# A decoder trunk on one core: the loads of its down projection in a written order, two homes for the sum Q + B21 and its load on GpSimd's queue, raw blocks in three loads

## The chip, the cores and the metric

The kernel runs on one NeuronCore of a Trainium2 chip. The metric is the device time of one execution in microseconds (us), and the time of a kernel is the median of its timed runs. A profile is one more execution, recorded instruction by instruction; its span runs from the first to the last recorded work.

Names: PE is the matrix engine (PEld loads its weights), DVE the vector engine, ACT the scalar engine, POOL is GpSimd, SP the engine that issues most DMAs. A home is a buffer in SBUF. Each engine takes its instructions in order; an engine that issues DMAs also does so in order, so a DMA that waits for its home holds back all that its engine issues behind it.

## The reference, cut to what matters

One layer of a hybrid decoder on 272 rows (16 meta tokens and 256 of the sequence) with a model width of 2048, in float32: a mixer of retention and mLSTM heads with its output projection, and then a gated FFN with a causal convolution of width 3. The change touches only the last product:

```python
u = rmsnorm(h, norm_ffn)
up = causal_dwconv(u @ w_up, ffn_conv_w, ffn_conv_b)   # 2048 -> 2 x 5632
gate, val = jnp.split(up, [FFN_DIM], axis=-1)
h = h + (jax.nn.silu(gate) * val) @ w_down             # 5632 -> 2048
return rmsnorm(h, norm_final)[:, N_META:]
```

## The kernel before, in words

**Precision.** Every weight and activation is split into a high part (a cast on ACT, tile `whi`) and a low part (a subtraction on DVE, tile `wlo`), and each product is three matmuls: high by high, high by low, low by high. `whi` and `wlo` have five buffers each.

**Two halves.** The FFN goes twice through an up projection (weights `wu`) and a down projection (weights `wd`), each time for half of the 5632 rows. In the trace the down projection of half 0 lies between 719 and 845 us, that of half 1 between 1098 and 1226 us.

**Blocks and steps.** A down projection has two blocks, b = 0 and b = 2, of 1024 columns each (two column blocks j of 512), and a block takes 11 steps q of 256 rows of `wd`. A plain step (q = 0, 9, 10; tile product L819 to L822) loads two weight tiles of 128 x 1024 (512 KB) from `wd`, splits them and has 12 matmuls of 512 columns for each j. A fast step (q = 1 to 8; `seven`, L824 to L855) is a Strassen-like scheme: seven products, 21 matmuls. For it the host gives `wd7`, four quarter matrices per step. The last block of half 1 takes its steps in the order 0, 1, 6, 2, 7, 3, 4, 5, 8, 9, 10, with 6 to 10 plain, and 7 to 10 in two parts.

**What a fast step reads.** Its raw block is a home `left[0]` or `left[1]` by turns (they lie in the tile `hT`), with four quarters of 128 x 512: quarter 0 is Q, a sum of quarter matrices, and 1 to 3 come from `wd7`. `ta` (L838, on DVE) is quarter 0 less quarters 1 and 2. `tb` is Q + B21. Q and Q + B21 are summed in DRAM ahead of time, by accumulating DMAs on POOL's queue during the up projection (class `Early`, L193 to L216; tile `kept`). Then four pairs of splits feed the seven products in this order: quarters 2 and 3; quarters 0 and 1; `ta`; `tb`. The weights' `whi` come from L766 (ACT), the `wlo` from L768 (DVE).

**Homes.** Beside `left` there are four homes for raw weights, `wraw0` and `wraw1`, two buffers each, shared by the up projection's tiles, the plain steps (one side or the other) and `ta` and `tb`, which take the two buffers of `wraw1`. So `ta` and `tb` have one home each.

**Ends of a block.** After the last fast step `share` adds and subtracts the products that belong to several outputs, and `onto` (L871) adds tiles `x` onto the hidden state `hn` by four DMAs on POOL's queue; four more follow when the plain sums leave PSUM (L964). At the end of half 1 the kernel loads `gfin` (1 MB, POOL's queue) and copies `a21`, which lies in the same memory as `left[1]` (L905), before the steps begin.

**Order.** The code is written step by step, and the framework's scheduler puts the instructions of each engine in order by simulated times; an `issue_after` pins one instruction behind another. In the code of before, the loads of a fast step are written inside `seven` (L833: quarter 0; L834: quarters 1 to 3; L837: `tb`), all on SP, and the plain loads (L126, by `load_step`) a step ahead; nothing is pinned there, and where they stand on SP is the scheduler's.

Of the kernel before, what the change touches and what calls it, by code (L numbers as in the profile page):

```python
# [13 lines left out]
ALU = mybir.AluOpType  # L14
PSUM = bass.MemoryType.PSUM

P = 128
# [68 lines left out]
def trunk(ctx: ExitStack, tc: tile.TileContext, io, out: bass.AP):  # L86
# [34 lines left out]
    def load_raw(src, shape, side=None):  # L121

        nonlocal last_load, loads
        raw = raw_home(shape, loads % 4 // 2 if side is None else side)
        loads += 1
        last_load = nc.sync.dma_start(raw, src)  # L126
        return raw
# [629 lines left out]
    for half in range(2):  # L757
# [66 lines left out]
        def seven(b, q, cs, ps, first, last, after, norm):  # L824


            nonlocal turn
            f = FAST.index(q)
            raw = left[turn]
            turn = 1 - turn  # L830

            kept = early[b, half * NQD + q].kept
            nc.sync.dma_start(raw[:, 0, :], kept[:, 0, :])  # L833
            nc.sync.dma_start(raw[:, 1:4, :], io["wd7"][b // 2, half * NQD + q][:, 1:4, :])  # L834
            ta, tb = (raw_home([P, 2, 512], 1) for _ in range(2))

            nc.sync.dma_start(tb[:, 0, :], kept[:, 1, :])  # L837
            nc.vector.tensor_tensor(out=ta, in0=raw[:, 0:1, :].to_broadcast([P, 2, 512]), in1=raw[:, 1:3, :], op=ALU.subtract)  # L838
            copied = None
            for w, to in (  # L840
# [3 lines left out]
                (tb[:, 0:1, :], ((A22, cs[1, 0], False, False),)),  # L844
# [24 lines left out]
        def onto(tt, b, x):  # L869

            nc.gpsimd.dma_start(block(tt, b), x, accum_op=ALU.add)  # L871

        def share(ps, b, final):
# [16 lines left out]
            onto(1, b + 1, x5)  # L890
# [17 lines left out]
        def load_step(b, q, side):  # L908

            return load_raw(io["wd"][b, half * NQD + q], [P, 2, 512], side)  # L910
# [7 lines left out]
        for b in (0, 2):  # L918
# [11 lines left out]
            raws = {}  # L930

            def load_plain(q):
                side = 0 if q == plain[0] or q not in steps[steps.index(fast[-1]) + 2 :] else plain.index(q) % 2
                for j in range(1 if q in alone else 2):
                    raws[q, j] = load_step(b + j, q, side)

            for n, q in enumerate(steps):

                if q in plain and (q, 0) not in raws:
                    load_plain(q)  # L940
                if n + 1 < len(steps) and steps[n + 1] in plain and q in fast:
                    load_plain(steps[n + 1])
                if q in fast:
# [4 lines left out]
                    if q == fast[-1]:  # L948
                        with tc.high_priority() if final else nullcontext():
                            share(ps, b, final)  # L950
                    continue
                for j in range(2):
                    if j == 1 and q in alone:
                        continue
                    w = split_step(raws[q, j])
                    for tt in range(2):
# [125 lines left out]
```

## Time and profile before

| | us |
|---|---|
| median of 3 runs | 1231.93 (1230.17 to 1232.15) |
| the profiled execution | 1235.55 |
| its span | 1233.8 |
| mean granted clock of PE (share of full speed) | 0.994 |
| down projection, half 0 | 719.2 to 844.6 |
| down projection, half 1 | 1098.2 to 1225.6 |

A row of a timeline gives start, duration, engine, line, operation, output and input tiles and, in brackets, how long the engine sat idle before it and what it waited for; rows of one kind in sequence are merged (x2). A row of the waits gives an engine's line and what it waited for: total us, times, longest. "SPq" and "POOLq" are the engines' queues of DMAs; the time of such a row is the issue and not the transfer.

### The profile page before, as it was taken

How to read it: one execution, taken by the hardware profiler on the slowest of the kernel's cores; microseconds unless marked ns; L12 is line 12 of the kernel's file. 1: busy time of each engine (PE TensorE's matmuls, PEld its weight loads, DVE VectorE, ACT ScalarE, POOL GpSimd, SP SyncE). 2: the span in 40 equal slices, each digit the busy share in tenths (PEclk: the TensorE clock that was granted, in tenths of full speed). 3: DMA queues.
4: the chain of work that ended last, by engine and by line, in shares of the span. 5: the costliest groups of instructions: out<-in, count | busy, mean ns of one | idle time of the engine just before them, and what ended most of it. 6: DMA issues, size and time to landing. Idle time of an engine off the chain costs nothing.

```text
span 1233.8 us, 22950 instructions
## 1 busy us (share of the span) xinstructions
PE 1207.8 (98%) x8947; PEld 1152.5 (93%) x8947; DVE 946.9 (77%) x1378; ACT 711.2 (58%) x973; POOL 248.8 (20%) x332
## 2 busy tenths in 40 slices
PE   9999999999999999999999999998999999999897
PEld 9999999999999999999999987678999999986686
DVE  8967878777766767788888789795877777769687
ACT  8747656565557546555555555654655555556564
POOL 0100022222222331232223100103232232200212
PEclk9999999999999999999999999999999999999899
DMA  7765677877786888787778857969988777856855
GB/s 273 273 205 163 209 227 224 229 230 219 229 226 187 254 235 246 218 235 231 223 231 230 264 180 239 247 234 284 284 247 232 225 229 229 219 185 219 236 202 180
DMA packets 101774, 281.64 MB, mean 228 GB/s; under 512 B 16160, under 2 KB 20384, under 8 KB 101536
## 3 DMA queue, kind: packets, MB, share of 16 engines
q1 hardware_dynamic: 84016, 246.66, 59.1%
q0 software_dynamic: 17072, 32.65, 16.7%
q8 instruction: 70, 1.15, 0.4%
q10 hardware_dynamic: 576, 0.85, 0.2%
q14 instruction: 40, 0.33, 0.1%
HBM read 268.59 MB, written 42.47 MB: 252 GB/s over the span
## 4 chain that ended last, share of the span: by engine, by line
PE 88%; DMA 6%; ACT 2%; DVE 2%; issue 1%; SPq 0%; DVEq 0%; ACTq 0%
PE mmps L149 25%; PE mmps L150 25%; PE mmps L152 25%; DMA wraw<-in_wd 2%; DMA wraw<-kept 2%; PE atps L819 1%; PE atps L820 1%; PE atps L822 1%; PE mmps L852 1%; PE mmps L853 1%; ACT whi L766 1%; PE mmps L855 1%; PE atps L852 1%; PE atps L853 1%; PE atps L855 1%
## 5 line engine op out<-in xcount | busy, mean ns | idle before, releaser
L140 ACT CAST whi<-wraw 128x1024 fp32r<-128x1024 f32 x346 | 361.7, 1048 | 356.5 <-PE mmps L150 217.4
L142 DVE TENSOR_TENSOR wlo<-wraw,whi 128x1024 fp32r<-128x1024 f32 x346 | 430.8, 1247 | 107.1 <-ACT whi L140 103.1
L149 PE MATMUL mmps<-uh,whi 128*128 128x258 f32 x1408 | 345.2, 283 | 1.8 <-ACT whi L140 1.8
L150 PE MATMUL mmps<-ul,whi 128*128 128x258 f32 x1408 | 344.9, 281 | 0.0
L149 PEld LDWEIGHTS mmps<-uh,whi 128*128 128x128 f32 x1408 | 265.2, 188 | 2.3 <-ACT whi L140 2.3
L150 PEld LDWEIGHTS mmps<-ul,whi 128*128 128x128 f32 x1408 | 266.5, 189 | 0.0
L149 PE MATMUL mmps<-xh,whi 128*128 128x272 f32 (+2 forms) x864 | 219.8, 288 | 0.0
L150 PE MATMUL mmps<-xl,whi 128*128 128x272 f32 (+2 forms) x864 | 218.4, 285 | 0.0
L152 PE MATMUL mmps<-uh,wlo 128*128 128x258 f32 x1408 | 197.9, 283 | 0.0
L152 PEld LDWEIGHTS mmps<-uh,wlo 128*128 128x128 f32 x1408 | 181.7, 189 | 0.0
L150 PEld LDWEIGHTS mmps<-xl,whi 128*128 128x128 f32 x864 | 162.8, 188 | 0.0
L149 PEld LDWEIGHTS mmps<-xh,whi 128*128 128x128 f32 x864 | 162.7, 188 | 0.1
L209 POOL TENSOR_TENSOR pace<-whi 128x1 f32<-128x1 f32 x87 | 51.4, 591 | 415.2 <-ACT whi L140 415.2
L152 PE MATMUL mmps<-xh,wlo 128*128 128x272 f32 (+2 forms) x864 | 126.9, 285 | 0.0
L152 PEld LDWEIGHTS mmps<-xh,wlo 128*128 128x128 f32 x864 | 114.6, 188 | 0.0
L695 DVE TENSOR_TENSOR cu<-mmps,rstd 128x258 f32<-128x258 f32 x88 | 37.5, 426 | 66.2 <-PE mmps L152 65.6
L766 ACT CAST whi<-wraw 128x1024 fp32r<-128x1024 f32 (+1 forms) x58 | 47.5, 835 | 51.2 <-DVE wraw L838 23.8
L768 DVE TENSOR_TENSOR wlo<-hT,whi 128x1024 fp32r<-128x1024 f32 x58 | 70.3, 1221 | 5.4 <-ACT whi L766 4.6
L766 ACT CAST whi<-hT 128x1024 fp32r<-128x1024 f32 x58 | 58.7, 1046 | 14.7 <-DMA hT<-in_wd 5.4
L150 PE MATMUL mmps<-mixl,whi 128*128 128x258 f32 x256 | 63.1, 283 | 0.0
L871 POOL DMA_DIRECT2D hn<-x x27 | 23.7, 1012 | 192.5 <-ACT x L878 162.8
L149 PE MATMUL mmps<-mixh,whi 128*128 128x258 f32 x256 | 62.5, 283 | 0.0
(270 smaller groups left out, 1790.5 us busy)
## 6 DMA issues: line engine op xcount, KB each, us to landing
wraw<-in_wu SPq DMA_DIRECT2D x176, 512.0 KB, 4.4
wraw<-in_wi SPq DMA_DIRECT2D x108, 512.0 KB, 4.4
hT<-in_wd SPq DMA_DIRECT2D x29, 768.0 KB, 5.2
wraw<-in_wo SPq DMA_DIRECT2D x32, 512.0 KB, 4.6
wraw<-in_wd SPq DMA_DIRECT2D x30, 512.0 KB, 4.7
kept<-in_wd SPq DMA_DIRECT2D x29, 512.0 KB, 6.5
kept<-in_wd POOLq DMA_DIRECT2D x58, 256.0 KB, 6.4
kept<-kept POOLq DMA_DIRECT2D x29, 256.0 KB, 5.4
```

Of the source, the lines that this page charges most:

```text
L140: nc.scalar.copy(hi, raw)
L142: nc.vector.tensor_tensor(out=lo, in0=raw, in1=hi.bitcast(F32), op=ALU.subtract)
L149: nc.tensor.matmul(ps, hi[:, k, :], xh(kk), start=kk == first, stop=False)
L150: nc.tensor.matmul(ps, hi[:, k, :], xl(kk), start=False, stop=False)
L152: nc.tensor.matmul(ps, lo[:, k, :], xh(kk), start=False, stop=kk == last)
L209: with tc.issue_after(nc.gpsimd.tensor_tensor(out=pace, in0=x, in1=x, op=ALU.add).ins):
L695: evacuated = nc.vector.tensor_tensor(out=u, in0=ps[:, :NQ], in1=rstd2, op=ALU.mult)
L766: copied = nc.scalar.copy(hi, x)
L768: return copied, nc.vector.tensor_tensor(out=lo, in0=x, in1=hi.bitcast(F32), op=ALU.subtract)
L852: nc.tensor.matmul(o, sh[:, f, m, :], hi[:, i, :], start=begin, stop=False)
L853: nc.tensor.matmul(o, sl[:, f, m, :], hi[:, i, :], start=False, stop=False)
L855: nc.tensor.matmul(o, sh[:, f, m, :], lo[:, i, :], start=False, stop=end)
```

## The change

- The loads of the down projection are written by themselves: `load_plain` (a plain step's tiles), `load_seven` (a raw block) and `load_sum` (`tb`). A table in the loop over the steps says after which step each stands: a raw block and a sum two steps ahead of their use; q = 9 after step 6, q = 10 after step 8; the next block's steps 1, 2 and 0 after steps 7, 8 and 9.
- All loads on SP are chained: each is issued after the one written before it (`begun`), so that their order is the program's.
- A raw block is three loads: quarters 2 and 3 (512 KB), quarter 1 (256 KB), and quarter 0, from `kept` (256 KB), where it was quarter 0 and then 1 to 3 (768 KB). The bytes are the same.
- `tb` is loaded from POOL's queue, into the two halves of one `wraw1` home by turns (even and odd steps). `ta` keeps one home, the other one. In a block that follows another in the same half, the loads of `tb` stand behind the last add of `share`.

```diff
-    def load_raw(src, shape, side=None):
+    def load_raw(src, shape):
...
         def seven(b, q, cs, ps, first, last, after, norm):
-            nonlocal turn
             f = FAST.index(q)
-            raw = left[turn]
-            turn = 1 - turn
-
-            kept = early[b, half * NQD + q].kept
-            nc.sync.dma_start(raw[:, 0, :], kept[:, 0, :])
-            nc.sync.dma_start(raw[:, 1:4, :], io["wd7"][b // 2, half * NQD + q][:, 1:4, :])
-            ta, tb = (raw_home([P, 2, 512], 1) for _ in range(2))
-
-            nc.sync.dma_start(tb[:, 0, :], kept[:, 1, :])
+            raw, ta, tb = homes.pop((b, q))
             nc.vector.tensor_tensor(out=ta, in0=raw[:, 0:1, :].to_broadcast([P, 2, 512]), in1=raw[:, 1:3, :], op=ALU.subtract)
...
+        def load(to, src):
+            nonlocal begun
+            with tc.issue_after(begun.ins) if begun else nullcontext():
+                begun = nc.sync.dma_start(to, src)
+
+        def load_plain(b, q, side, n=2):
+            for j in range(b, b + n):
+                raws[j, q] = raw_home([P, 2, 512], side)
+                load(raws[j, q], io["wd"][j, half * NQD + q])
+
+        def load_seven(b, q):
+            nonlocal turn
+            raw = left[turn]
+            turn = 1 - turn
+            load(raw[:, 2:4, :], io["wd7"][b // 2, half * NQD + q][:, 2:4, :])
+            load(raw[:, 1, :], io["wd7"][b // 2, half * NQD + q][:, 1, :])
+            load(raw[:, 0, :], early[b, half * NQD + q].kept[:, 0, :])
+            homes[b, q] = raw
+
+        def load_sum(b, q):
+            tb = sums_home[1][:, FAST.index(q) % 2, :][:, None, :]
+            with tc.issue_after(shared.ins) if shared else nullcontext():
+                nc.gpsimd.dma_start(tb[:, 0, :], early[b, half * NQD + q].kept[:, 1, :])
+            homes[b, q] = homes[b, q], sums_home[0], tb
...
+            if b == 0:
+                load_plain(b, 0, 0)
+                load_seven(b, 1)
+                load_seven(b, 2)
+            sums_home = [raw_home([P, 2, 512], 1) for _ in range(2)]
+            load_sum(b, 1)
+            load_sum(b, 2)
+            for q in steps:
...
+                if final:
...
+                else:
+                    if q == 6:
+                        load_plain(b, 9, 0)
+                    if q in range(1, 7):
+                        load_seven(b, q + 2)
+                        load_sum(b, q + 2)
+                    if q == 8:
+                        load_plain(b, 10, 1)
+                    if b == 0:
+                        if q in (7, 8):
+                            load_seven(2, q - 6)
+                        elif q == 9:
+                            load_plain(2, 0, 0)
```

How the instructions stand now, at three places. In these listings `hT` is the raw block, `wraw` a home, `in_wd` the weights in DRAM (`wd` or `wd7`), and `kept_8_87` and the like the sums of one step.

SP in half 0, from the last fast step's block to the next block's plain step q = 0; before:

```order
L833 DMA hT<-kept_1_88 128x512
L834 DMA hT<-in_wd 128x1536
L837 DMA wraw_9471<-kept_8_87 128x512
L833 DMA hT<-kept_2_89 128x512
L834 DMA hT<-in_wd 128x1536
L837 DMA wraw_9643<-kept_1_88 128x512
L126 DMA wraw_9552<-in_wd 128x1024
L126 DMA wraw_9554<-in_wd 128x1024
L126 DMA wraw_9604<-in_wd 128x1024
L126 DMA wraw_9606<-in_wd 128x1024
L126 DMA wraw_9941<-in_wd 128x1024
L126 DMA wraw_9943<-in_wd 128x1024
```

and with the change:

```order
L907 DMA hT<-kept_8_87 128x512
L907 DMA hT<-in_wd 128x1024
L907 DMA hT<-in_wd 128x512
L907 DMA hT<-kept_1_88 128x512
L907 DMA wraw_9517<-in_wd 128x1024
L907 DMA wraw_9519<-in_wd 128x1024
L907 DMA hT<-in_wd 128x1024
L907 DMA hT<-in_wd 128x512
L907 DMA hT<-kept_2_89 128x512
L907 DMA wraw_9556<-in_wd 128x1024
L907 DMA wraw_9558<-in_wd 128x1024
```

The sums of steps 8 and 1 (`wraw<-kept`) are no longer in SP's row; q = 10 (9552 and 9554 before, 9517 and 9519 now) stands ahead of the next block's step 2, and q = 0 (9604, 9606; now 9556, 9558) behind it. The loads 9941 and 9943 (q = 9 of the next block) follow six steps later now.

SP at the start of half 1's down projection, before:

```order
L126 DMA wraw_13250<-in_wd 128x1024
L837 DMA wraw_13289<-kept_12_96 128x512
L126 DMA wraw_13252<-in_wd 128x1024
L126 DMA wraw_13587<-in_wd 128x1024
L126 DMA wraw_13589<-in_wd 128x1024
L833 DMA hT<-kept_14_98 128x512
L834 DMA hT<-in_wd 128x1536
L833 DMA hT<-kept_13_97 128x512
L834 DMA hT<-in_wd 128x1536
L837 DMA wraw_13332<-kept_13_97 128x512
```

and with the change:

```order
L907 DMA wraw_13238<-in_wd 128x1024
L907 DMA wraw_13240<-in_wd 128x1024
L907 DMA hT<-in_wd 128x1024
L907 DMA hT<-in_wd 128x512
L907 DMA hT<-kept_12_96 128x512
L907 DMA hT<-in_wd 128x1024
L907 DMA hT<-in_wd 128x512
L907 DMA hT<-kept_13_97 128x512
L907 DMA hT<-in_wd 128x1024
L907 DMA hT<-in_wd 128x512
L907 DMA hT<-kept_14_98 128x512
```

Here 12, 13 and 14 are steps 1, 2 and 3. Step 3's block stood ahead of step 2's; now they follow in their order, each behind q = 0. Step 1's block, which stood far ahead of q = 0, stands behind it.

POOL over half 0's down projection, before:

```order
L209 TENSOR_TENSOR pace<-whi 128x1
L214 DMA kept_15_99<-in_wd 128x512
L871 DMA hn<-x_5921 128x512 x14
L209 TENSOR_TENSOR pace<-whi 128x1
L214 DMA kept_16_100<-in_wd 128x512
```

and with the change:

```order
L928 DMA wraw_9138<-kept_1_80 128x512
L928 DMA wraw_9138<-kept_2_81 128x512
L209 TENSOR_TENSOR pace<-whi 128x1
L214 DMA kept_15_99<-in_wd 128x512
L928 DMA wraw_9138<-kept_3_82 128x512
L928 DMA wraw_9138<-kept_4_83 128x512
L928 DMA wraw_9138<-kept_5_84 128x512
L928 DMA wraw_9138<-kept_6_85 128x512
L928 DMA wraw_9138<-kept_7_86 128x512
L928 DMA wraw_9138<-kept_8_87 128x512
L863 DMA hn<-x_5921 128x512 x4
L928 DMA wraw_9609<-kept_1_88 128x512
```

POOL's row had only the adds onto `hn` between the last sums in DRAM; the loads of `tb` now fill it, the next block's behind the four adds of `share`.

48 lines of the change are left out of this document (23 added, 25 removed).

## The prediction

> **What bounds the kernel now.** I read the head of the page first, then the windows over the two stretches of the down projection, and only then who waits there.
>
> ```profile
> span 1233.8 us, 22950 instructions
> PE 1207.8 (98%) x8947; PEld 1152.5 (93%) x8947; DVE 946.9 (77%) x1378; ACT 711.2 (58%) x973; POOL 248.8 (20%) x332
> ```
>
> PE is the bound as a whole, and the change gives it the same matmuls. So a gain can only come out of time in which PE stands still or runs at a low clock inside the down projection. The price of one matmul of 512 columns is read off PE's timeline: between these two rows lie 18 of them.
>
> ```profile
> 724.81 0.39 PE L852 MATMUL atps<-whi,sh 128*128 128x512 f32 x1
> ...
> 729.01 0.39 PE L852 MATMUL atps<-whi,sh 128*128 128x512 f32 x1
> ```
>
> 4.20 / 18 = 0.2333 us. A fast step (21 matmuls) is 4.90 us of PE, a plain step (24) 5.60. The windows by stage (columns: window and its length, then busy time of PE, PEld, DVE, ACT and POOL, granted clock, DMA share, GB/s):
>
> ```profile
> 719.20:844.60 125.40, 116.84 (x483) 89.95 (x481) 101.17 (x101) 70.75 (x84) 12.32 (x14) 0.99 0.75 233
> 725.00:755.00 30.00, 30.00 (x130) 24.12 (x130) 27.06 (x26) 19.68 (x22) 0.00 (x0) 1.00 0.59 205
> 770.00:780.00 10.00, 7.95 (x33) 5.51 (x31) 4.39 (x5) 3.34 (x5) 4.40 (x5) 1.00 1.05 250
> 780.00:785.00 5.00, 4.17 (x11) 3.30 (x12) 3.04 (x3) 4.65 (x7) 1.75 (x2) 0.66 0.98 197
> 1098.20:1225.60 127.40, 119.56 (x514) 93.73 (x513) 101.41 (x106) 71.93 (x95) 21.41 (x23) 0.97 0.68 214
> 1160.00:1170.00 10.00, 6.24 (x17) 4.60 (x16) 3.62 (x4) 5.49 (x7) 2.79 (x4) 0.68 0.92 215
> 1170.00:1225.00 55.00, 55.00 (x257) 45.22 (x256) 47.60 (x51) 32.40 (x48) 13.86 (x14) 1.00 0.59 186
> ```
>
> Half 0 has 480 matmuls: 480 × 0.2333 = 112.0 of 125.4 us, so 13.4 are lost. Half 1 has 465 of 512 columns and 48 of 256, taken at half the price: 108.5 + 5.6 = 114.1 of 127.4, so 13.3 are lost. Together 26.7 us; nothing of it lies in the last block (1170 to 1225, PE full). A part is clock: after long gaps PE was granted 0.66 and 0.68, which costs 4.17 × 0.34 = 1.4 us and 6.24 × 0.32 = 2.0 us. The rest is waiting, by the view of waits on PEld (total us, times, longest), half 0 first:
>
> ```profile
> PEld atps L819 <- ACT whi L140: 6.2, 5, 3.1
> PEld mmps L852 <- ACT whi L766: 4.4, 6, 1.1
> PEld mmps L149 <- ACT whi L140: 2.3, 1, 2.3
> PEld atps L852 <- ACT whi L766: 1.6, 3, 0.9
> ```
>
> and half 1:
>
> ```profile
> PEld mmps L852 <- ACT whi L766: 5.3, 7, 1.1
> PEld atps L819 <- ACT whi L140: 5.1, 2, 4.2
> PEld atps L852 <- ACT whi L766: 2.7, 5, 1.2
> ```
>
> L819 and L149 are plain steps and the exit to the up projection: I call these the **transitions**. L852 is the fast steps: the **runs**. PEld waits somewhat longer than PE idles, since it stands a matmul ahead: 14.5 against 13.4 − 1.4 = 12.0 (factor 0.83), 13.1 against 13.3 − 2.0 = 11.3 (0.86). So the transitions lose 8.5 × 0.83 + 1.4 = 8.5 and 5.1 × 0.86 + 2.0 = 6.4, sum 14.9; the runs 6.0 × 0.83 + 8.0 × 0.86 = 11.9.
>
> **The runs, part one: two homes for the sum.** SP's and ACT's timelines show what paces them:
>
> ```profile
> 752.17 0.32 SPq L837 DMA_DIRECT2D wraw<-kept  x1
> ...
> 758.32 0.32 SPq L837 DMA_DIRECT2D wraw<-kept  x1
> ...
> 763.96 0.32 SPq L837 DMA_DIRECT2D wraw<-kept  x1
> ```
>
> ```profile
> 764.15 0.62 ACT L766 CAST whi<-wraw 128x512 fp32r<-128x512 f32 x1 [1.48 <-DMA wraw<-kept]
> 771.00 1.05 ACT L140 CAST whi<-wraw 128x1024 fp32r<-128x1024 f32 x1 [3.85 <-DMA wraw<-in_wd]
> ...
> 779.73 1.04 ACT L140 CAST whi<-wraw 128x1024 fp32r<-128x1024 f32 x1 [3.70 <-DMA wraw<-in_wd]
> ```
>
> The sum has one home, so its next load can only start when the cast and the subtraction of this step have read it; it lands, ACT casts it (764.15), and the ring closes: 6.15 and 5.64 us a step, where PE needs 4.90. On DVE, the ends of step 2 and step 8, and two steps between without that wait:
>
> ```profile
> 728.47 1.83 DVE L768 TENSOR_TENSOR wlo<-wraw,whi 128x1024 fp32r<-128x1024 f32 x2 [0.17 <-ACT whi L766]
> ...
> 740.07 1.83 DVE L768 TENSOR_TENSOR wlo<-wraw,whi 128x1024 fp32r<-128x1024 f32 x2
> ...
> 745.37 1.83 DVE L768 TENSOR_TENSOR wlo<-wraw,whi 128x1024 fp32r<-128x1024 f32 x2
> ...
> 764.80 0.69 DVE L768 TENSOR_TENSOR wlo<-wraw,whi 128x512 fp32r<-128x512 f32 x1 [0.87 <-ACT whi L766]
> ```
>
> Step 2 ends at 730.3, step 8 at 765.5: 35.2 / 6 = 5.87 us a step. Undisturbed it is 745.37 − 740.07 = 5.30. DVE is thus slower than PE either way, and lives on its lead. Step 1's matmuls begin at 724.8, so step 8's begin at 724.8 + 34.3 = 759.1, and its last product, the one with the sum, needs DVE by about 763.8 (18 matmuls for its turn, and two more ahead of the one that reads wlo). Before: 765.5, 1.7 late. With two homes: 730.3 + 6 × 5.30 = 762.1, 1.7 early; any pace under (763.8 − 730.3) / 6 = 5.58 leaves PE without a stall. The run of the second block has the same form.
>
> Whether 5.30 is reached hangs on the sum's new queue. POOL has the load to issue once DVE has read that home, two steps ahead. Rows for its price (issue on POOL min/median/max ns; landings of POOL's transfers in us):
>
> ```profile
> L214 POOL DMA_DIRECT2D kept<-in_wd x58: 796/823/1005, 143.7 to 1068.0; - x58
> ...
> kept<-in_wd POOLq DMA_DIRECT2D x58, 256.0 KB, 6.4
> kept<-kept POOLq DMA_DIRECT2D x29, 256.0 KB, 5.4
> ```
>
> ```profile
> DMA to landing us min/median/max: 4.2/7.3/12.5
> ```
>
> The last row is the adds onto the hidden state (tile hn, 719 to 860), the nearest POOL transfers in time, with a busier window than the runs have. The ring over two steps is then: 0.15 from DVE to POOL (my estimate), 0.82 issue, landing, cast 0.62, subtraction 0.69, some 0.2 between them, or 2.5 + landing. At 6.4 that is 8.9 for two steps, 4.45 a step, under DVE's 5.30; it begins to bind at a landing of 8.1 and to cost PE at 8.7. From below the price is nothing; from above 12.5, the second rival. I take 6.4, since the runs' DMA share (0.59) is not that of 770 to 780. SP loses 29 short loads and gains 29 (raw blocks in three pieces), nothing; POOL has 0.00 us of work in 725 to 755, so its 29 × 0.82 = 24 us lie beside everything else.
>
> **The runs, part two: order at the start of half 1.** SP issues step 3's block first, then step 2's:
>
> ```profile
> 1096.88 0.33 SPq L833 DMA_DIRECT2D hT<-kept  x1
> ...
> 1099.62 0.43 SPq L834 DMA_DIRECT2D hT<-in_wd  x1
> ```
>
> ```profile
> 1108.39 1.23 DVE L838 TENSOR_TENSOR wraw<-hT 128x1024 f32<-128x1024 f32 x1 [6.01 <-DMA hT<-in_wd]
> ```
>
> DVE idles 6.01 us for the block that went second, landing 8.8 after its issue. In the fixed order step 2's last two columns go first, the rest right behind the copy that empties its home, and step 3's follows. With a normal landing (5.2 for 768 KB) DVE starts step 2 some 3.5 earlier and the lead is as in half 0: stall 0. So of the 11.9 of the runs I take 11.0; the remainder is for waits of 0.2 to 0.3 us that the change doesn't touch.
>
> **The transitions.** SP now issues: the next block's step 1, q10, step 2, q0. Before, all plain loads stood behind three waits for the sum:
>
> ```profile
> 767.00 17.75 SPq L126 DMA_DIRECT2D wraw<-in_wd  x6
> ```
>
> q10's two loads went at 767.0 and later, and ACT sat 3.85 and 3.70 us for them and for q0 (rows above). Now q10 follows when DVE has left the homes of step 8: about 761.4 and 762.1. PE reaches q10 at 764.0 + 5.6 = 769.6 and its second column block at 772.4, which gives 7 us for landing and cast: enough. q0's first half is wanted by 775.2, its second by 778. Between 761.4 and then DMA must move q10, step 2 and q0 (3 MB) and the four adds onto the hidden state (1 MB). By the queue rows
>
> ```profile
> q1 hardware_dynamic: 84016, 246.66, 59.1%
> q0 software_dynamic: 17072, 32.65, 16.7%
> ```
>
> SP's queue takes 0.591 × 1233.8 / 246.66 = 2.96 us a MB, POOL's 6.3: 8.9 + 6.3 = 15.2 us, so to 776.6, cast 1.05 later. That is on the edge: 0 to 1.5 us of stall at each of the three transitions, and the clock stays up, since the runs have waits of that size (longest 1.1 and 1.2) at a clock of 0.99 to 1.00 over the stretch. I take 1.3 each: 14.9 − 3.9 = 11.0.
>
> **Sum.** 11.0 + 11.0 = 22.0 us, from span 1233.8 to 1211.8. The profiled execution took 1235.55, 3.6 above the median of 1231.93; the stalls that go are the same in both, so 1231.9 − 22.0 = 1209.9, say 1210. If all went: 1231.9 − 26.7 = 1205.2. The covers: POOL's issue hides behind an idle POOL; without it, 0.82 a fast step, 24 us. When the ring is gone, DVE is late next (5.30 against 4.90), by 0.4 us a step, which its lead pays for six steps.
>
> **Rivals.** *First, the transitions stay.* DMA is full there (1.05 in 770 to 780), and an earlier issue does not make 4 MB shorter; q0 stands behind step 2's MB. Against it: from 725 to 755 the share is 0.59, so there is room ahead. Then only the runs' 11.0 and some 2 of the transitions are gained: 1219. The Trainium skill, DMA: Bandwidth & Descriptors, section "Issuing engines are not separate DMA queues", says that transfers run on the same 16 engines whoever starts them, so that a second issuer saves issue time alone; the trace agrees at 1.05, and by that rule it is this rival.
>
> *Second, slower: the sums on POOL's queue land late.* If each lands as the slowest add does, 12.5, the ring is (12.5 + 2.5) / 2 = 7.5 a step. The three full runs then stall 6 × 7.5 − 33.5 (763.8 − 730.3) = 11.5 each, 34.5; the last block has only five fast steps with two plain ones between (four intervals, 30 us against 28.0 of PE and a lead of 4.1) and none. 34.5 − 22.8 that the rest saves (26.7 less the 3.9) = +12, 1244. It decides from a mean landing of about 11.2 on (6.85 a step). For it speaks that the adds reach it; against, that 87 POOL transfers from DRAM have medians of 5.4 and 6.4. The Trainium skill, SBUF — State Buffer, "Who interferes with whom", puts a DMA that stalls under VectorE down to GpSimd starved of its port while it builds descriptors, and advises a hardware queue; it infers that tensor_tensor leaves the port needed free. The row of L214 (823 ns, at most 1005) agrees with the latter in this kernel.
>
> *Third, no change:* the order that SP is given makes each plain load wait for a raw block ahead of it, and what the runs gain is lost at transitions and at the entry from the up projection, where steps 1 and 2 now go behind q0. They land about 6 us after it and PE wants step 1 a plain step later; within 2 us of before, 1232.
>
> **How the numbers follow.** Forecast 0.63 (own range 1206 to 1214), first rival 0.24 (1214 to 1223), second 0.07, third 0.06. The range of 8 in 10 is 1206 to 1222. A difference under 0.2%, 2.5 us, cannot be told from none. Faster 0.87, same 0.05, slower 0.08.
>
> **What would show it.** Right: no wait of ACT L766 on a kept load; DVE's end of step 2 to step 8 31 to 33 us; ACT's wait for in_wd under 5 us a half; no granted clock under 0.9 inside the two stretches, which take 114 to 117 us each; the sums land in 5 to 7.5. Wrong: stalls over 2 us at q0 (first rival); landings beyond 9 and stalls at L852 that grow from step to step (second); new stalls at the entries of the halves (third).

## The result, and the profile after

The changed kernel takes 1221.97 us (median of 6 runs, 1220.31 to 1224.28) against 1231.45 for the kernel before, measured beside it. The ratio is 0.9923, with a 95% interval of 0.9907 to 0.9939: faster by 9.5 us, where 22 were forecast; 1221.97 lies outside the forecast's own range of 1206 to 1214. In three later groups of runs, on two chips, the same pair gave 0.9899 (0.9876 to 0.9922), 0.9885 (0.9869 to 0.9900) and 0.9897 (0.9876 to 0.9918), or 12 to 14 us. The profiled execution took 1222.59 us; the head of its page:

```profile
span 1220.8 us, 23064 instructions
PE 1202.5 (99%) x8947; PEld 1154.5 (95%) x8947; DVE 943.0 (77%) x1378; ACT 712.9 (58%) x973; POOL 270.1 (22%) x361
```

The waits on PEld in the changed kernel, half 0 and then half 1 (total us, times, longest):

```profile
PEld mmps L149 <- ACT whi L140: 3.1, 1, 3.1
PEld atps L819 <- ACT x L1000: 2.6, 1, 2.6
...
PEld atps L819 <- ACT x L1000: 4.2, 1, 4.2
PEld mmps L844 <- ACT whi L766: 0.7, 1, 0.7
PEld atps L844 <- ACT whi L766: 0.3, 1, 0.3
```

Before, these lists held 14.5 and 13.1 us. The fast steps (L852 then, L844 now) have fallen from 6.0 and 8.0 us to 0 and 1.0. The plain steps and the exit to the up projection have kept most of theirs: 8.5 and 5.1 then, 5.7 and 4.2 now. The release named `x L1000` is a copy that stands behind the cast of q0 (the next block's step q = 0) in ACT's row; PE starts 0.55 us after that cast ends. What ACT itself waited for is a load, as its timeline shows further down.

The windows of the changed kernel (busy time of PE, PEld, DVE, ACT, POOL, granted clock, DMA share, GB/s; the share of full engines comes out at up to 1.1 in these profiles):

```profile
718.90:836.00 117.10, 114.96 (x492) 92.33 (x491) 100.39 (x102) 71.03 (x83) 19.97 (x28) 0.99 0.77 240
770.00:775.00 5.00, 5.00 (x22) 3.76 (x20) 1.29 (x2) 0.00 (x0) 0.91 (x2) 1.00 1.08 300
775.00:780.00 5.00, 2.86 (x10) 2.20 (x10) 1.98 (x2) 3.85 (x6) 1.80 (x3) 0.83 1.03 250
780.00:785.00 5.00, 5.00 (x20) 3.98 (x19) 4.31 (x5) 4.60 (x6) 1.73 (x2) 0.83 1.07 168
835.00:840.00 5.00, 2.93 (x22) 2.61 (x20) 0.00 (x0) 0.24 (x1) 0.85 (x1) 1.00 1.08 302
1091.50:1212.60 121.10, 117.04 (x515) 94.39 (x513) 99.83 (x106) 72.45 (x95) 31.06 (x34) 0.97 0.74 228
1150.00:1155.00 5.00, 2.88 (x7) 2.31 (x8) 2.13 (x2) 4.00 (x7) 1.97 (x3) 0.54 0.88 211
1155.00:1160.00 5.00, 5.00 (x19) 3.99 (x18) 4.31 (x5) 4.03 (x6) 1.57 (x2) 0.78 1.05 262
```

The two down projections take 117.1 and 121.1 us in these windows, where they took 125.4 and 127.4. The first pair is not like for like: the window of 117.1 us ends ahead of the gap at the exit, and matmuls of the up projection already lie in it. Taken from the first matmul of the down projection to that of the up projection's second half tile (719.21 to 847.58 before, 718.94 to 840.86 now), half 0 is 6.5 us shorter and half 1 is 6.3, together 12.8 of the 13.0 by which the spans differ. What is left stands at three places, and PE's timeline names them: the first tile of q0 in half 0, the second half tile of the up projection behind half 0 (the exit), and q0 in half 1. I call the way from one block to the next, with its q0, the passage.

```profile
777.24 0.50 PE L819 MATMUL atps<-whi,mh 128*128 128x512 f32 x1 [2.14 <-ACT x L1000]
...
840.86 0.39 PE L149 MATMUL mmps<-uh,whi 128*128 128x258 f32 x1 [2.93 <-ACT whi L140]
...
1152.12 0.80 PE L819 MATMUL atps<-whi,mh 128*128 128x512 f32 x1 [3.76 <-ACT x L1000]
```

By the measure of the prediction (0.83 and 0.86 of the waits, and the low clock: (2.86 + 5.00) × 0.17 = 1.3 in half 0, 2.88 × 0.46 + 5.00 × 0.22 = 2.4 in half 1), the runs fell from 11.9 to 0.9 us, and the transitions from 14.9 to 5.7 × 0.83 + 1.3 + 4.2 × 0.86 + 2.4 = 12.0. So in this execution 11.0 us came from the runs, as forecast, and 2.9 from the transitions in place of 11.0. Together 13.9, near the 13.0 by which the spans differ.

The same kernel was profiled three times more (e5, e9 and e13 below), and the places change from one execution to the next. Waits on PEld in us, the time lost to a low clock behind the gaps, and the gains by the same measure:

| | first | e5 | e9 | e13 |
|---|---|---|---|---|
| q0, half 0 | 2.6 | 0 | 2.7 | 0.2 |
| exit | 3.1 | 2.8 | 2.1 | 3.4 |
| q0, half 1 | 4.2 | 2.8 | 2.9 | 4.8 |
| fast steps | 1.0 | 3.4 | 3.4 | 2.8 |
| low clock | 3.7 | 1.3 | 2.9 | 5.3 |
| gained in the runs | 11.0 | 9.1 | 9.0 | 9.6 |
| gained in the transitions | 2.9 | 8.9 | 5.5 | 2.5 |
| span less than before | 13.0 | 17.6 | 14.5 | 11.7 |

So the exit and the passage of half 1 stall in all four, the passage of half 0 only in two. The runs keep 2.8 to 3.4 us of waits in three of the four, and the transitions gain 2.5 to 8.9 us where 11.0 were forecast.

The runs. DVE's timeline with the ends of step 2 and step 8 of the first block:

```profile
728.21 1.83 DVE L768 TENSOR_TENSOR wlo<-wraw,whi 128x1024 fp32r<-128x1024 f32 x2 [0.18 <-ACT whi L766]
...
759.93 1.83 DVE L768 TENSOR_TENSOR wlo<-wraw,whi 128x1024 fp32r<-128x1024 f32 x2
```

Step 2 ends at 730.04 and step 8 at 761.76, or 5.29 us a step; 762.1 and 5.30 were forecast.

The transition in half 0, in the first profile. SP's timeline and ACT's:

```profile
761.18 0.93 SPq L907 DMA_DIRECT2D wraw<-in_wd  x2
762.17 0.90 SPq L907 DMA_DIRECT2D hT<-in_wd  x2
763.16 0.70 SPq L907 DMA_DIRECT2D hT<-kept  x1
763.96 1.99 SPq L907 DMA_DIRECT2D wraw<-in_wd  x2
```

```profile
775.65 1.04 ACT L140 CAST whi<-wraw 128x1024 fp32r<-128x1024 f32 x1 [6.84 <-DMA wraw<-in_wd]
```

q10 goes at 761.18 (761.4 was forecast), then step 2's raw block, then q0 at 763.96. So q0 is issued 9.4 us earlier than before (773.33), and still its first tile can be cast only at 775.65: 11.7 us after its issue, behind the megabyte of step 2, with the adds and two sums beside it on engines that are full (1.08). In e5 and e13 the same load, in the same place, is cast 9.3 and 9.7 us after its issue (772.91 and 773.48), which is just in time: this passage is on the edge. That of half 1 is beyond it, with q0 cast 11 to 13 us after its issue in all four profiles. That is what the experiments had to explain: is it the engines, or what stands ahead in the queue?

### The profile page after: what moved, and what is told of

The parts are those of the page before. It is cut to its first block, busy times and chain, and to the rows that moved or that the text cites. A ratio compares the mean times of both kernels' runs of the same rounds, so it can differ in the third digit from the quotient of the medians.

```text
span 1220.8 us, 23064 instructions
## 1 busy us (share of the span) xinstructions
PE 1202.5 (99%) x8947; PEld 1154.5 (95%) x8947; DVE 943.0 (77%) x1378; ACT 712.9 (58%) x973; POOL 270.1 (22%) x361
## 4 chain that ended last, share of the span: by engine, by line
PE 94%; DMA 4%; DVE 1%; ACT 1%; issue 0%; DVEq 0%; SPq 0%; ACTq 0%
PE mmps L149 25%; PE mmps L152 25%; PE mmps L150 25%; DMA wraw<-in_wd 2%; PE mmps L844 2%; PE mmps L845 2%; PE mmps L847 2%; PE atps L845 1%; PE atps L844 1%; PE atps L819 1%; PE atps L822 1%; PE atps L820 1%; PE atps L847 1%; DMA wraw<-in_wu 1%; DMA hT<-kept 1%; PE atps L442 1%
## 5 line engine op out<-in xcount | busy, mean ns | idle before, releaser
L766 ACT CAST whi<-hT 128x1024 fp32r<-128x1024 f32 x58 | 59.7, 1050 | 15.2 <-DMA hT<-kept 4.6
L768 DVE TENSOR_TENSOR wlo<-wraw,whi 128x1024 fp32r<-128x1024 f32 (+1 forms) x58 | 53.2, 953 | 1.9 <-PE mmps L847 0.8
```

The lines of the kernel that those rows point to most:

```text
L766: copied = nc.scalar.copy(hi, x)
L768: return copied, nc.vector.tensor_tensor(out=lo, in0=x, in1=hi.bitcast(F32), op=ALU.subtract)
```

## The experiments

Four groups (e1 to e4, e5 to e8, e9 to e12, e13 to e16), each on one chip, with the kernel before beside them. All ratios are against that kernel, with 95% intervals.

| run | edit to the changed kernel | median us | ratio |
|---|---|---|---|
| e1 | q0 ahead of step 2's block | 1214.81 | 0.9870 (0.9835 to 0.9904) |
| e2 | sides of the second up projection shifted | 1213.54 | 0.9851 (0.9824 to 0.9879) |
| e3 | both | 1210.11 | 0.9822 (0.9796 to 0.9848) |
| e4 | without the adds of block 0 | 1215.54 | 0.9863 (0.9830 to 0.9896) |
| e5 | none | 1218.99 | 0.9899 (0.9876 to 0.9922) |
| e6 | one home for the sum | 1239.39 | 1.0072 (1.0047 to 1.0097) |
| e7 | sum loaded by SP | 1221.77 | 0.9915 (0.9883 to 0.9947) |
| e8 | (kernel before) two homes alone | 1227.09 | 0.9958 (0.9945 to 0.9972) |
| e9 | none | 1218.63 | 0.9885 (0.9869 to 0.9900) |
| e10 | both, as e3 | 1211.23 | 0.9826 (0.9812 to 0.9840) |
| e11 | gfin later | 1214.96 | 0.9873 (0.9851 to 0.9894) |
| e12 | both and gfin later | 1209.79 | 0.9814 (0.9800 to 0.9828) |
| e13 | none | 1219.41 | 0.9897 (0.9876 to 0.9918) |
| e14 | raw block in two loads | 1222.48 | 0.9919 (0.9905 to 0.9934) |
| e15 | as e1 | 1213.44 | 0.9843 (0.9825 to 0.9861) |
| e16 | as e2 | 1215.05 | 0.9860 (0.9839 to 0.9880) |

### The passage between two blocks: q0 ahead of step 2's block (e1, e15)

```diff
-                        if q in (7, 8):
-                            load_seven(2, q - 6)
+                        if q == 7:
+                            load_seven(2, 1)
                         elif q == 9:
                             load_plain(2, 0, 0)
+                            load_seven(2, 2)
```

> The changed kernel with one edit: at the two passages from block 0 to block 2, the next block's plain step q0 (1 MB) is loaded ahead of that block's raw block of step 2 (1 MB) instead of behind it. Theory A (order): q0's tiles landed 11 to 12 us after their issue because a megabyte that nobody needed yet stood ahead of them; the stalls at q0 (2.3 and 3.9 us) and the low clock behind them (some 1.2 and 2.1) fall to 1 or less each, and the time falls by 5 to 8 us, to 1214 to 1217. Theory B (the 16 DMA engines are full at the passage, whatever the order): the stall moves to the raw block that is now last, or stays; within 2 us of 1222.

> The changed kernel with q0 ahead of step 2's raw block, now beside the changed kernel on one chip. Theory A (order): the two passages between blocks give 3 to 6 us; the stall at the exit to the up projection (2.8 to 3.1) stays. Theory B (full engines): within 2 us.

Measured: 1214.81, and on the chip of e13 to e16 1213.44 against 1219.41 for the changed kernel, 6.0 us less. SP, ACT and the windows in e1:

```profile
761.57 3.20 SPq L907 DMA_DIRECT2D wraw<-in_wd  x4
764.82 1.05 SPq L907 DMA_DIRECT2D hT<-in_wd  x2
765.97 0.84 SPq L907 DMA_DIRECT2D hT<-kept  x1
```

```profile
769.36 1.05 ACT L140 CAST whi<-wraw 128x1024 fp32r<-128x1024 f32 x1 [1.59 <-DMA wraw<-in_wd]
771.72 1.05 ACT L140 CAST whi<-wraw 128x1024 fp32r<-128x1024 f32 x1 [1.30 <-DVE wlo L142]
```

```profile
770.00:775.00 5.00, 5.00 (x23) 4.04 (x22) 3.58 (x3) 2.54 (x4) 1.76 (x4) 1.00 1.09 285
775.00:780.00 5.00, 5.00 (x23) 4.00 (x22) 0.70 (x1) 2.85 (x4) 2.62 (x4) 1.00 1.10 278
```

q0's two tiles are cast at 769.36 and 771.72, six us before those of the first profile (in e15 at 768.21 and 771.30, some five before those of e13). The DMA engines are as full as ever (1.09 and 1.10), and PE neither stops nor loses its clock there. By itself that shows little, since the changed kernel did not stop there in e13 either. At a q0 it stopped only in half 1; e13's windows in half 0 and half 1:

```profile
775.00:780.00 5.00, 5.00 (x23) 4.02 (x22) 2.98 (x3) 4.54 (x8) 3.40 (x4) 1.00 1.11 260
1150.00:1155.00 5.00, 1.86 (x4) 1.49 (x5) 1.23 (x1) 2.92 (x4) 1.62 (x2) 0.71 0.90 219
```

It is half 1 that decides: the wait at q0 there is 1.1 us in e1 and 0.7 in e15, against 2.8 to 4.8 in the four profiles of the changed kernel. The 6.0 us of e15 stand on intervals that do not overlap. So full engines alone do not cause the stall; they make the order count. Theory B falls. The block that now stands last costs next to nothing (1.2 and 0.5 us of waits in the fast steps of e1 and e15, not more than the changed kernel has), because PE wants it a plain step and a fast step later.

### The exit to the up projection (e2, e16)

In the changed kernel SP and ACT read so at the exit:

```profile
821.99 0.93 SPq L907 DMA_DIRECT2D wraw<-in_wd  x2
823.72 1.47 SPq L126 DMA_DIRECT2D wraw<-in_wu  x2
825.24 0.50 SPq L203 DMA_DIRECT2D kept<-in_wd  x1
827.95 30.41 SPq L126 DMA_DIRECT2D wraw<-in_wu  x11
```

```profile
839.76 1.04 ACT L140 CAST whi<-wraw 128x1024 fp32r<-128x1024 f32 x1 [5.47 <-DMA wraw<-in_wu]
```

Weight homes are taken in pairs, two on each side, and the count stands so that the up projection's first tile takes its first half from the side that q9 leaves and its second half from the side of q10. The two loads at 823.72 are the first half and one that is wanted fourth; the second half goes at 827.95, when q10 has been split, behind these two and 512 KB for `kept`. It is cast at 839.76. The edit shifts the count by three:

```diff
+        loads += 3 * half
         mh = midp.tile([P, 2 * len(PLAIN), SEQ], F32R, name="mh")
```

> The changed kernel with one edit: the turn of the two sides of weight homes is shifted for the second up projection, so that its first tile's two halves both take the homes that q9 leaves, and not one of them a home of q10. Theory A (order and homes): the stall of 3.1 us behind the first half tile of the up projection goes, 1219. Theory B (full engines): the second half lands as late as before, 1222.

> The changed kernel with the shifted sides of the second up projection, beside the changed kernel on one chip. Theory A (order): the stall at the exit goes, and only that: 2.5 to 3.5 us. If it gives 5 or more, the edit reaches beyond the exit, and the passages vary from build to build.

Measured: 1213.54 where 1219 was expected (without the changed kernel beside it), and 1215.05 against 1219.41 in the fourth group, 4.4 us less. The stall at the exit is gone in both profiles, where the four of the changed kernel have 2.1 to 3.4 us of it. The gain is above the 2.5 to 3.5 expected, but the intervals of e13 and e16 are 4 to 5 us wide and overlap by a little, and the profiled execution of e13 waited 3.4 us at the exit and ran at a clock of 0.51 behind it (840 to 845). So 4.4 doesn't need another cause, and none is shown.

### Both (e3, e10)

> The changed kernel with the edits of the two runs before together. Theory A: the two gains add up, 8 to 11 us, 1211 to 1214. Theory B: 1220 to 1222.

> The changed kernel with q0 ahead of step 2's raw block and the shifted sides of the second up projection, beside the changed kernel on one chip. Theory A (order and homes at the passages): 8 to 11 us under the changed kernel. Theory B (full engines, and the earlier gains were the chip's): within 3 us of it.

Measured: 1210.11, just under the range of e3, and 1211.23 against 1218.63 on one chip, 7.4 us less. That is under the expected 8 to 11, and under the sum of the single edits (10.4 in another group). PEld's waits in e10, half 0 and half 1, and the windows at its exit (with the shifted sides the kernel has a line more, so L845 here is L844 above):

```profile
PEld mmps L845 <- ACT whi L767: 1.2, 2, 0.6
...
PEld mmps L845 <- ACT whi L767: 0.4, 1, 0.4
PEld atps L820 <- ACT x L1002: 0.2, 1, 0.2
```

```profile
825.00:830.00 5.00, 5.00 (x23) 4.00 (x23) 3.97 (x5) 2.26 (x3) 2.10 (x3) 1.00 1.07 292
830.00:835.00 5.00, 5.00 (x35) 4.56 (x34) 2.79 (x3) 3.89 (x6) 3.50 (x4) 1.00 1.08 306
835.00:840.00 5.00, 5.00 (x44) 5.00 (x43) 1.65 (x2) 1.19 (x2) 1.98 (x3) 1.00 1.07 327
```

All that is left is 1.8 us of waits, with DMA shares of 1.07 and 1.08 and PE full.

### The price of the adds (e4)

```diff
         def onto(tt, b, x):
+            if b < 2:
+                return None
             return nc.gpsimd.dma_start(block(tt, b), x, accum_op=ALU.add)
```

> The changed kernel without the eight accumulating DMAs (2 MB) that add the sums of block 0 onto the hidden state in each half: this part of the result is left out. Both theories expect a gain at the passages, since less is moved there; it prices the adds. By the time that their queue took per MB (5.6 us) the four that come before q0 lands cost 5 to 6 us of the engines: Theory B expects the stalls at q0 to go wholly (1214), Theory A expects half of them to stay, since q0 still stands behind the raw block (1217 to 1218).

Measured: 1215.54. There was no changed kernel in that group; by the ratios (0.9863 against 0.9885 to 0.9923) it is 3 to 7 us faster, with an interval (0.9830 to 0.9896) that reaches into theirs. The waits at q0 are 0.5 us in half 0, which the changed kernel has at times too, and 1.2 in half 1, under all four of its values; Theory A had half of them stay, Theory B none. So the adds carry their part: without them q0 lands nearly in time even behind the raw block. The stall in half 1 takes both, the full engines and the megabyte ahead; taking away either ends most of it. A kernel cannot move the adds ahead, since what they add ends just there.

### Which part of the change gave the runs (e5 to e8)

> The changed kernel itself, on the same chip as the three runs beside it, as their measure. All theories: 1222, the time found for it (1220 to 1224). If it comes out lower here, part of the gains of the runs before it was the chip's.

Measured: 1218.99, three us under the first measure and under the 1220 to 1224 expected; its ratio is the first of the three later ones of the result above.

One home (e6): a step's sum is loaded behind the reading of the step before, so each step reads the sum that belongs to the next one, with the same loads and waits.

```diff
-            tb = sums_home[1][:, FAST.index(q) % 2, :][:, None, :]
+            tb = sums_home[1][:, 0, :][:, None, :]
```

> The changed kernel with one edit: the sum Q + B21 has one home again, still loaded from GpSimd's queue, all else as changed. Theory A (one home closes a ring of load, cast and subtraction in each fast step): with the landing of 5.3 us that these loads have in the changed kernel and 1.4 for cast and subtraction the ring is 6.7 to 6.9 us a step; each of the three full runs then stalls 6 x 6.8 - 33.5 = 7 us, the last block little: 21 us slower than the changed kernel, 1236 to 1246. Theory B (the order of the loads is what ended the stalls in the runs): within 3 of the changed kernel.

Measured: 1239.39, 20.4 us over e5. The size was as expected, its place was not. ACT's wait for the sum in half 0, DVE at the ends of steps 2 and 8 of the first block, and the waits on PEld in half 0:

```profile
ACT whi L766 <- DMA wraw<-kept: 23.1, 10, 6.8
```

```profile
728.29 1.83 DVE L768 TENSOR_TENSOR wlo<-wraw,whi 128x1024 fp32r<-128x1024 f32 x2 [0.18 <-ACT whi L766]
...
763.34 1.82 DVE L768 TENSOR_TENSOR wlo<-wraw,whi 128x1024 fp32r<-128x1024 f32 x2
```

```profile
PEld atps L844 <- ACT whi L766: 8.9, 8, 3.0
PEld atps L819 <- ACT x L1000: 4.4, 1, 4.4
```

From 730.12 to 765.16 it is 5.84 us a step, not 6.8: the rate of the kernel before. The landing of 5.3 us in the expectation is not that of these loads; they land in 3.5 us (median, 725 to 760). Where the expectation had 7 us of stall in this run, it stalls 2.2, but DVE ends step 8 3.4 us later than in the changed kernel, and with it the homes of q10 and the loads of q0: the passage waits 4.4 and runs at a low clock behind it (0.66 from 780 to 785). The fast steps of the four blocks wait 2.2, 7.8, 4.9 and 6.3 us, where 7, 7, 7 and little were expected, and the mean clock is 0.988 to 0.993 against 0.996 to 0.997 in e5, some 7 us of PE's 1202 by my estimate. So the ring is real, and that its price came out at 21 is luck. Theory B falls: the fixed order without the second home is slower than the kernel before.

The sum on SP (e7):

```diff
-            with tc.issue_after(shared.ins) if shared else nullcontext():
-                nc.gpsimd.dma_start(tb[:, 0, :], early[b, half * NQD + q].kept[:, 1, :])
+            load(tb[:, 0, :], early[b, half * NQD + q].kept[:, 1, :])
```

> The changed kernel with one edit: the sum is loaded by SP, in its fixed order behind its step's raw block, into the two homes by turns. Theory A (the queue is indifferent, the homes matter): within 2.5 us of the changed kernel, no stall in the runs. Theory B (the sums hold back what stands behind them on SP, since each waits for its home): stalls in the runs come back, 4 us or more slower.

Measured: 1221.77 against 1218.99; the intervals (0.9883 to 0.9947, 0.9876 to 0.9922) overlap, and which queue loads the sum makes no difference that these runs tell. Its profile has 6.1 us of waits in the fast steps (the longest 1.6), where the changed kernel has 1.0 to 3.4, so "no stall in the runs" is not what came, and a cost of 2 to 3 us on SP is not excluded.

Two homes alone in the kernel before (e8):

```diff
-            ta, tb = (raw_home([P, 2, 512], 1) for _ in range(2))
+            ta, tb = sums_home[0], sums_home[1][:, f % 2, :][:, None, :]
```

with `sums_home` taken once for a block, as in the changed kernel.

> The kernel before with one edit: two homes by turns for the sum, still loaded by SP in the scheduler's order. Theory A (two homes alone are the gain of the runs): the waits of ACT for the sum go, DVE's pace falls from 5.9 to 5.3 us a step, and 6 to 9 us of the runs' 11.9 are gained; the late block at the start of half 1 and the passages stay: 1223 to 1226. Theory B (without the fixed order the freed time is lost elsewhere): within 3 of 1232.

Measured: 1227.09, 5.2 us under the kernel before beside it (1232.27), one above the range expected. PEld in half 0 and in half 1 of e8:

```profile
PEld atps L819 <- ACT whi L140: 7.1, 4, 3.1
PEld mmps L852 <- ACT whi L766: 1.8, 3, 0.8
...
PEld atps L819 <- ACT whi L140: 5.5, 2, 3.3
PEld mmps L852 <- ACT whi L766: 2.3, 4, 0.8
```

DVE ends step 2 at 730.58 and step 8 at 762.30, 5.29 us a step, the pace of the changed kernel. The waits at L852 fell from 14.0 to 4.3 us, those at L819 (12.6) are what the plain steps and the exit had before (13.6). So by the waits (9.7 us, where the changed kernel brings 10.6 to 13.0) the second home is the greater part of what the runs gained, and it brings nothing to the passages. By the medians it is 5.2 us.

### Half 1, and the lead that DVE brings to a passage (e11, e12)

In half 1 of the changed kernel DVE's step 2 reads:

```profile
1091.98 0.54 POOL L894 DMA_DIRECT2D gfin<-in_gfin  x1 [17.55 <-PE mmps L152]
...
1100.05 1.22 DVE L830 TENSOR_TENSOR wraw<-hT 128x1024 f32<-128x1024 f32 x1 [0.85 <-DMA hT<-kept]
...
1102.47 1.83 DVE L768 TENSOR_TENSOR wlo<-wraw,whi 128x1024 fp32r<-128x1024 f32 x2
```

POOL's `gfin` (1 MB) goes 0.65 us ahead of SP's first load for this block (1092.63), quarter 0 of step 2 lands late, and step 2 ends at 1104.30. PE began step 1 at 1097.12, so 7.2 us before (7.0 to 7.3 in the other profiles of this kernel); in half 0 it was 730.04 − 724.54 = 5.5. DVE carries these 1.7 us to step 8 (its end by the pace of 5.29 is 1136.0), and so to the homes that q10 waits for. The edit of e11 puts the load behind the sum of step 5:

```diff
-            nc.gpsimd.dma_start(gfin, io["gfin"])
...
+                        summed = load_sum(b, q + 2)
+                        if half == 1 and q == 3:
+                            with tc.issue_after(summed.ins):
+                                nc.gpsimd.dma_start(gfin, io["gfin"])
```

> The changed kernel with one edit: the 1 MB load of gfin goes behind the sum of step 5 in half 1's first block, and no longer ahead of that block's first loads. Theory C (half 1's passage is the longest because DVE's lead over PE is 1.7 us shorter there, since its first blocks land behind gfin): step 2 ends by 5.5 to 6 us after step 1's first matmul instead of 7.2, the homes for q10 come free 1.5 us earlier, and the stall at q0 in half 1 falls by 1.5 to 4 us with its cold clock: 2 to 4 us faster than the changed kernel. Rival (the passage's length is a matter of its own traffic, whatever the lead): same within 1.5 us.

Measured: 1214.96 against 1218.63 (e9), 3.7 us less, with intervals that overlap (0.9851 to 0.9894, 0.9869 to 0.9900). The first half of the mechanism reads as expected in DVE's timeline of e11:

```profile
1097.73 1.83 DVE L768 TENSOR_TENSOR wlo<-wraw,whi 128x1024 fp32r<-128x1024 f32 x2 [0.17 <-ACT whi L766]
```

Step 2 ends at 1099.56, 5.5 us behind step 1's first matmul (1094.07), and PE's gap at q0 in half 1 is 1.7 us, where e9 has 2.4 and the first profile 3.8. That `gfin` takes the lead is shown. That the lead makes the stall is not: the changed kernel's gap varies from 2.4 to 4.3 us at the same lead. Its share of the time is not settled either.

> The changed kernel again, as the measure on this chip for the three runs beside it: 1217 to 1224.

> The changed kernel with all three edits: q0 ahead of step 2's raw block, shifted sides, gfin late. If the lead and the order are what is left: 1206 to 1209, at most 2 us above the time without any stall in the down projections (1205). If the full engines are: as the run with two edits.

Measured: 1218.63 (e9) and 1209.79 (e12). The three edits together are 8.8 us under the changed kernel and 22.7 under the kernel before (1232.48). From the two edits of e10 (1211.23) e12 is not told apart; it ends 0.8 us above the range expected, and waits 1.3 us at q0 in half 1, where e10 waits 0.2. Either is faster than both kernels, with the same computation.

### Raw blocks in two loads (e13, e14)

```diff
-            load(raw[:, 2:4, :], io["wd7"][b // 2, half * NQD + q][:, 2:4, :])
-            load(raw[:, 1, :], io["wd7"][b // 2, half * NQD + q][:, 1, :])
+            load(raw[:, 1:4, :], io["wd7"][b // 2, half * NQD + q][:, 1:4, :])
```

> The changed kernel again, as the measure on this chip for the three runs beside it: 1217 to 1224.

> The changed kernel with one edit: a raw block comes in two loads (quarters 1 to 3, then quarter 0) and not in three, in the same fixed order. Theory A (the passages' order and the homes decide): within 2.5 us of the changed kernel. Rival (the first product of a step needs only quarters 2 and 3, and their earlier landing carries DVE's lead): the cast of quarters 2 and 3 starts 1 us later in a step that waits for its block, 2 to 4 us slower.

Measured: 1219.41 and 1222.48. The changed kernel is 3.1 us the faster by the medians, but its six executions reach from 1215.88 to 1223.93 and the intervals overlap. It leans to the rival and is not settled; a loss by the three loads is unlikely.

## Why the prediction was wrong, step by step

**What bounds the kernel:** right. 26.7 us were lost in the down projections, and 12.8 of the 13.0 us that the span lost come out of them; the best variant is 22.7 us under the kernel before.

**The runs, two homes:** right in mechanism, and nearly in size: 11.0 us forecast, 11.0 found in the first profile and 9.0 to 9.6 in the three others. DVE's pace (5.30 forecast, 5.29 found), the end of step 8 (762.1 and 761.76) and the absence of stalls under 5.58 us a step came as worked out in the first block, and in the second block of the first profile. In the others the run of half 0's second block keeps 1.8 to 3.2 us of waits, so "the same form" did not hold for it every time; why is not shown. e8 shows that the second home alone does most of the gain, e6 that nothing else in the change replaces it. The landing of the sums was taken at 6.4 us and is 4.2 (3.2 in the run from 724 to 757), and their issue at 0.82 and is 0.54, which only adds cover; the step from DVE to POOL, taken at 0.15, is 0.30 (730.04 to 730.34).

**The order at the start of half 1:** right in kind, since step 2 is no longer late by 6 us. That "the lead is as in half 0" was wrong by 1.7 us: `gfin`'s megabyte, which the prediction had not listed among that window's loads, was issued behind SP's first blocks before (1098.60, after 1096.88) and goes ahead of them now. The run itself stalled 1.0 us in the waits; that the rest was paid at the passage is argued and not shown.

**The transitions:** here it failed. "0 to 1.5 us of stall at each of the three transitions, and the clock stays up", with 1.3 taken for each, was to leave 3.9 of 14.9 us, a gain of 11.0; the changed kernel's first profile keeps 12.0, a gain of 2.9, and the three others gain 2.5 to 8.9. Half 0's passage alone met that step, in two executions of four. Three parts of it were missed:

- *q0's place in the queue.* The sum of 15.2 us from 761.4 put the end of q0 at 776.6. Its tiles could be cast at 775.65 and 778.17, so the sum was right to 1.5 us, and was then read too kindly: PE was to have q0 by 775.2, which with the cast means landed by 774.1. The sum also left out the two loads of the next block's sums, 0.5 MB that start behind the adds, and half 1, where q0 came 11 to 13 us after its issue, was never reckoned by itself. What mattered, and the sum took as given, is that a megabyte for a step that PE reaches some 10 us later (a plain step and a fast one) is ahead of q0 in SP's order; e15 takes it away and gains 6.0 us.
- *The exit.* The prediction gave it the 1.3 us of a passage and did not look at its loads. What waits there is the up projection's second half tile, whose home is one of q10's, and whose load stands behind two others and 512 KB for `kept`. e16 takes that away and gains 4.4 by the medians.
- *The clock.* The gap of 2.1 us at q0 in half 0 was followed by a clock of 0.83, and the one of 3.8 in half 1 by 0.54 and 0.78: 3.7 us that the step had at zero (1.3 to 5.3 in the other profiles).

**The sum:** "the stalls that go are the same in both" did not hold in the first measure, where the span fell by 13.0 us and the median by 9.5. Over all four groups the spans fell by 14.2 us on average and the medians by 12.5. The profiled execution of before stood 3.6 above its median, at a clock of 0.994 where others of that kernel had up to 0.999, so a part of what it lost behind its gaps was probably its own; one profile of before cannot show it.

**The rivals:** the first (the transitions stay, 1219) is what came, 1218.6 to 1222.0, with its sign, stalls over 2 us at q0 (2.1 and 3.8 in the first profile). Its ground was half right. The engines are full there (1.08), and q0 stands behind step 2's megabyte; but that "an earlier issue does not make 4 MB shorter" decides nothing as long as the megabyte that PE wants next goes first. The Trainium skill, DMA: Bandwidth & Descriptors, section "Queues, rings and completion order", says that SP's transfers go through one row of rings, and that an engine takes turns between rows; so what SP issues later waits behind what it issued earlier, while GpSimd's loads get their turn. The trace agrees with the first: in the passage q0 took 11.7 us to its cast in third place (9.3 and 9.7 in e5 and e13) and 6 in second. The second rival (late sums) did not come: their median landing is 4.2 us, under all its bounds, and only those that fall into a passage reach 10 to 11.5. By the prediction's own condition the third (no change) is out as well, since a fixed order made nothing worse at the entries.

## What to carry to other kernels

When DMA engines are full over a stretch, the question is not only whether the bytes fit but which of them the next stall needs: write down, for every load in that stretch, when it is wanted, and issue in that order. A load's issue time is set by its home, and the home by the lead of the engine that reads it last; a run with few stalls can still have spent its lead, and may pay at the next passage (in e6 DVE ended step 8 3.4 us later, and PE waited 4.4 us at q0 behind it). A gap that a profile shows may cost a second time through the clock, and that part varies between executions, so gains added up from one profile can miss either way: 22 forecast against 9.5, 2.5 to 3.5 against 4.4. Profile the same kernel more than once before a stall of two us is put down to a cause: here one stood in two executions of four.

## What the runs showed that was not expected

- The time of the changed kernel goes with the granted clock from execution to execution. The six of e13 are 1215.88, 1218.02, 1218.91, 1219.92, 1222.22 and 1223.93 us, at mean clocks of 0.998, 0.997, 0.997, 0.995, 0.993 and 0.992. The kernels without long gaps (e10, e12) have 0.998 or 0.999 in all of theirs, and spread by 1.7 and 2.9 us. It is not the clock alone: the kernel before, beside e9, has an execution of 1230.31 us at 0.993 and one of 1232.61 at 0.996.
- The gap alone does not settle what the clock does. In the changed kernel's profile the clock stayed at 1.00 behind the gap of 2.9 us at the exit (windows from 835 to 845), and fell to 0.83 behind the 2.1 us at q0. In e9 it is the other way round: 1.00 behind a gap of 2.2 us at q0 (775 to 785), and 0.66 behind one of 1.9 at the exit (840 to 845). The Trainium skill, TensorE: Matmul & The Clock Gate, Part 1 (the HAM clock gate), has a window of some 3.4 us that runs free of the program; with that, it is the place of a gap in the window that decides, which would suit these rows. No run here shows the window itself.
- The sums that GpSimd issues land sooner in the run from 724 to 757 than SP's loads of the same size there: 3.2 us against 4.3 and 4.6 (medians of six). The queue is not shown to be the reason, since the sum takes 3.8 us there from SP in e7 and 3.8 from GpSimd in e1. Issued on an idle POOL the sums cost 0.54 us, where the accumulating loads cost 0.82.
